# Seven block products in place of eight in the SwiGLU down-projections of a two-layer hybrid trunk

## The chip, the cores and the metric

The kernel runs on one core of one Trainium2 chip. The metric is the device time of one execution in microseconds (us), as a median of several runs. TensorE (PE) multiplies, VectorE (DVE) and ScalarE (ACT) work on rows of 128 partitions, GpSimd (POOL) does elementwise work and issues accumulating DMAs, SyncE (SP) issues plain loads.

## The reference

Two layers over x of 512 positions by 1024 features, in float32. Each layer is a SwiGLU stage, a token-mixing stage (recurrent branch, short convolution, sparse attention) and a second SwiGLU stage:

```
def swiglu(x, w_gate_up, w_down):
    g, u = jnp.split(x @ w_gate_up, 2, axis=-1)
    return (jax.nn.silu(g) * u) @ w_down

for l in range(DEPTH):                                   # DEPTH = 2
    x = x + 0.5 * swiglu(rms_norm(x, ffn1_norm[l]), ffn1_w_gate_up[l], ffn1_w_down[l])
    x = x + token_mixing(rms_norm(x, mix_norm[l]), ...)
    x = x + 0.5 * swiglu(rms_norm(x, ffn2_norm[l]), ffn2_w_gate_up[l], ffn2_w_down[l])
return rms_norm(x, final_norm)
```

D_MODEL is 1024 and D_FF is 2816, so a down-projection maps 22 chunks of 128 hidden rows to 8 chunks of 128 features, and there are four of them.

## The kernel before

Features lie on the partitions, the 512 positions are the columns. x is held as 8 tiles of 128x512. Float32 accuracy is had with three matmuls for each product of two 128-wide operands (`mm3`, L390 to L392): every operand is cut into a rounded part `hi` and a remainder `lo`, and hi by hi, hi by lo and lo by hi are added up in PSUM.

**The stream of weights.** `Stream` (from L210) brings all weights as 496 units of 128x1024 (eight 128x128 tiles) in the order in which TensorE will use them. A unit is loaded into a raw buffer by SP (L231; five buffers, RAWB), and cut: ScalarE writes minus the raw weight into `wlo` (L251) and the rounded weight into `whi` (L252), and an accumulating DMA issued by POOL (L253) moves `wraw` onto `wlo`. There are three pairs of cut buffers (CUTB): a unit's cut begins when the unit three places ahead of it has been used up.

**A SwiGLU stage** (`ffn`, L517) takes 22 hidden chunks in two halves of 11. Each hidden chunk has a gate and an up projection, each a `chunk` of 8 k-steps (24 matmuls of 512 columns, one weight unit). VectorE evacuates them (L530, L539), ScalarE applies silu (L532), POOL multiplies gate and up (L542), and `cut` (L412 to L418) makes hi and lo of the hidden chunk. After each half come 8 down chunks, one for each x tile, of 11 k-steps (33 matmuls); VectorE adds half of each result to x (L555). After the second half each finished x tile goes to the next norm at once (`Norm.add`): hi and lo of the scaled x (L443 on ScalarE, L444 on VectorE), its square (L451) and the sum of squares on POOL (L460). The next stage's matmuls need seven of its eight x tiles before the first may start (`chunk`, `v_task`).

**The order.** `Sched` runs a list schedule at build time: every task is a generator that yields operations with a cost, a priority and waits; the operation with the lowest priority number that is ready goes next on its engine, and the instructions are issued in this order. The cuts of weights have priority -1e6 and so go ahead of all else on their engines; evacuations of PSUM get a bump of -100; all else has the order number of its task. On the chip each engine then works through its own list in order.

**PSUM** has eight banks: three of kind a (chunks), two s, two t, one o (attention, norms and the value projection). SBUF holds 66 slots of 128x512 (`G`, NSLOT), eight of them x.

Of the kernel before, what the change touches and what calls it, by code (L numbers as in the profile page):

```python
# [20 lines left out]
P = 128  # L21
# [18 lines left out]
NHU = 496  # L40
RAWB, CUTB = 5, 3
NSLOT = 66
# [5 lines left out]
TOPK_AT = 40  # L48

# [159 lines left out]

class Stream:  # L210


    def __init__(self, nc, sch, pool, wall):
        self.nc, self.s, self.pool, self.wall = nc, sch, pool, wall
        self.n = wall.shape[0]
        self.parts, self.order, self.avail = {}, [], 0
        self.raw, self.cut = Res(RAWB), Res(CUTB)

    def task(self, gate):
        for j in range(self.n):  # L220
            if j == 1:
                yield gate
            yield self.raw
            box = {}
            pieces = 4 if j == 0 else 1
            w = 1024 // pieces

            def dma():
                if "raw" not in box:
                    box["raw"] = self.pool.tile([P, 1024], F32, name="wraw", tag="wraw", bufs=RAWB)  # L230
                self.nc.sync.dma_start(box["raw"][:, i * w:(i + 1) * w], self.wall[j][:, i * w:(i + 1) * w])  # L231

            for i in range(pieces):
                yield "sp", 1.46 if j else 0.6, dma, {}
                self.s.spawn(self._cut(j, box["raw"], i * w, w), -1e6 + j)
                if pieces > 1:
                    yield 0.7

    def _cut(self, j, raw, off, w):
        yield 2.0  # L240
        if off == 0:
            yield self.cut
            self.parts[j] = (self.pool.tile([P, 1024], F32R, name="whi", tag="whi", bufs=CUTB),
                             self.pool.tile([P, 1024], F32R, name="wlo", tag="wlo", bufs=CUTB))
        hi, lo = (t[:, off:off + w] for t in self.parts[j])
        src = raw[:, off:off + w]
        if j == 0:
            yield ACT(w, lambda: self.nc.scalar.copy(hi, src))
            yield DVE(w, lambda: self.nc.vector.tensor_sub(lo, src, hi.bitcast(F32)))
        else:  # L250
            yield ACT(w, lambda: self.nc.scalar.mul(lo, src, -1.0))  # L251
            yield ACT(w, lambda: self.nc.scalar.copy(hi, src))  # L252
            yield "pool", 1.0, lambda: self.nc.gpsimd.dma_start(lo, src, accum_op=ALU.add), {}  # L253
            yield 4.0
        if off + w == 1024:
            self.s.release(self.raw)
        self.avail += w // P
# [7 lines left out]
    def half(self, key):  # L265
        j = len(self.order) // 8
        self.order += [key + (r,) for r in range(8)]
        return self.parts.pop(j)

    def tile(self, key):  # L270
        j, r = divmod(len(self.order), 8)
        self.order.append(key)
        hi, lo = self.parts[j]
        if r == 7:
            del self.parts[j]
            self.s._at(self.s.t + 0.7, lambda: self.s.release(self.cut))
        return hi[:, r * P:(r + 1) * P], lo[:, r * P:(r + 1) * P]
# [3 lines left out]
def trunk_kernel(ctx: ExitStack, tc: tile.TileContext, wall, x_in, pos_in, cols_in, out):  # L281
# [10 lines left out]
    W = Stream(nc, sch, wp, wall)  # L292
# [223 lines left out]

    def ffn(name, l, u, xs, nxt):  # L517

        hid = [Part() for _ in range(2 * HF)]
        mid = [Event() for _ in range(KT)]  # L520
        new = [[x, Event()] for x, _ in xs]

        def pair(c, prio):
# [11 lines left out]
            def u_task():  # L535
                ps = yield from chunk((name + "u", l, c), u.u)
                yield u.rev
                t2 = G()
# [3 lines left out]
                yield POOL(S, lambda: O.tensor_mul(t2, box["t"], t2))  # L542
# [607 lines left out]
```

## Time and profile before

| what | us |
|---|---|
| median of three runs | 2962.79 (2962.65 to 2963.1) |
| the profiled execution, its own time | 2961.89 |
| span of the profiled execution, first to last instruction | 2960.0 |
| TensorE busy | 2897.5 (98%), 12720 matmuls |
| VectorE, ScalarE, POOL busy | 955.2 (32%), 1499.6 (51%), 927.6 (31%) |
| mean granted clock of TensorE | 0.987 |

The profile is of one execution, 1.9 us of which lie outside the span. A matmul row gives a start and a modelled duration; matmuls overlap, so the pace is read from the distance of the starts and not from the durations. Times in rows are us from the span's start, means are in ns.

### The profile page before, as it was taken

Reading aid. Unit: us, or ns where it says so; the run is one execution under the profiler, and the core shown is the slowest. Engines: PE = TensorE matmul, PEld = TensorE weight load, DVE = VectorE, ACT = ScalarE, POOL = GpSimd, SP = SyncE. Lnnn points to the kernel's source line nnn. Section 1 sums busy time; section 2 is a strip of 40 time slices with the busy share of each in tenths; the row PEclk is TensorE's granted clock in tenths of the full one; section 3 lists DMA queues with packets and bytes.
Section 4 is the critical chain, followed back from the end, with each engine's and each line's share of the span. In section 5 each row is a group of like instructions: output and inputs, shape, how many; then the busy total and the mean of one; then the engine's idle time right before and its main releaser. Section 6 shows DMA issues by size and latency. Waiting matters only on the chain.

```text
span 2960.0 us, 32761 instructions
## 1 busy us (share of the span) xinstructions
PE 2897.5 (98%) x12720; PEld 2358.5 (80%) x12720; DVE 955.2 (32%) x1699; ACT 1499.6 (51%) x1930; POOL 927.6 (31%) x923
## 2 busy tenths in 40 slices
PE   8999999799999999999999999988999999999998
PEld 6888887678888888888888888877788888888886
DVE  5311148944312222111111111599361231211111
ACT  5534457666533455434544345567664334544443
POOL 2212254543222232212322123646332222322222
PEclk9999999899999999999999999999999999999999
DMA  7888886566688888888888888856657888888885
GB/s 213 188 194 185 188 196 159 132 162 145 138 191 192 190 185 185 187 189 185 193 185 192 184 193 185 199 135 157 159 130 165 186 187 190 186 186 190 191 185 128
DMA packets 145818, 526.29 MB, mean 178 GB/s; under 512 B 16192, under 2 KB 16832, under 8 KB 145664
## 3 DMA queue, kind: packets, MB, share of 16 engines
q0 software_dynamic: 71360, 259.82, 49.0%
q1 hardware_dynamic: 73584, 263.23, 27.7%
q8 instruction: 100, 1.64, 0.2%
q10 hardware_dynamic: 720, 1.17, 0.1%
q14 instruction: 54, 0.44, 0.1%
HBM read 262.53 MB, written 2.10 MB: 89 GB/s over the span
## 4 chain that ended last, share of the span: by engine, by line
PE 90%; DVE 7%; ACT 1%; issue 1%; POOL 1%; DMA 1%; SPq 0%; DVEq 0%; ACTq 0%; POOLq 0%
PE psa L390 29%; PE psa L392 29%; PE psa L391 29%; DVE g L706 1%; DVE m L705 1%; DVE g L731 1%; DVE g L771 1%; PE pst L915 1%; DVE g L770 0%; DVE g L699 0%; DVE g L791 0%; DVE g L728 0%; PE pso L930 0%; DVE g L793 0%; PE pso L931 0%
## 5 line engine op out<-in xcount | busy, mean ns | idle before, releaser
L390 PE MATMUL psa<-g,whi 128*128 128x512 f32 x3920 | 1560.5, 398 | 43.3 <-DVE xr L726 27.9
L391 PE MATMUL psa<-g,whi 128*128 128x512 f32 x3920 | 1556.6, 397 | 6.1 <-POOL g L418 5.8
L392 PE MATMUL psa<-g,wlo 128*128 128x512 f32 x3920 | 1556.0, 397 | 0.8 <-DMA wlo<-wraw 0.8
L251 ACT ACTIVATE wlo<-wraw 128x1024 fp32r<-128x1024 f32 x495 | 524.6, 1060 | 1235.1 <-PE psa L392 1226.3
L390 PEld LDWEIGHTS psa<-g,whi 128*128 128x128 f32 x3920 | 744.6, 190 | 218.6 <-DVE xr L726 23.9
L391 PEld LDWEIGHTS psa<-g,whi 128*128 128x128 f32 x3920 | 744.6, 190 | 177.4 <-POOL g L418 6.7
L392 PEld LDWEIGHTS psa<-g,wlo 128*128 128x128 f32 x3920 | 744.3, 190 | 175.6 <-DMA wlo<-wraw 1.6
L253 POOL DMA_DIRECT2D wlo<-wraw x495 | 429.3, 867 | 1231.7 <-ACT wlo L251 1148.2
L252 ACT CAST whi<-wraw 128x1024 fp32r<-128x1024 f32 x495 | 511.3, 1033 | 0.0
L542 POOL TENSOR_TENSOR g<-g 128x512 f32<-128x512 f32 x88 | 114.2, 1297 | 358.4 <-DVE g L539 347.0
L416 DVE TENSOR_TENSOR g<-g 128x512 fp32r<-128x512 f32 x142 | 102.7, 723 | 267.3 <-ACT g L414 267.0
L539 DVE TENSOR_TENSOR g<-psa,g 128x512 f32<-128x512 f32 x88 | 60.8, 691 | 379.4 <-PE psa L392 379.4
L555 DVE SCALAR_TENSOR_TENSOR x<-psa,x 128x512 f32<-128x512 f32 x64 | 44.3, 692 | 384.3 <-PE psa L392 384.3
L414 ACT CAST g<-g 128x512 fp32r<-128x512 f32 x174 | 107.8, 619 | 77.3 <-DVE g L731 32.4
L530 DVE TENSOR_TENSOR g<-psa,g 128x512 f32<-128x512 f32 x88 | 60.9, 692 | 180.4 <-PE psa L392 180.3
L841 POOL TENSOR_TENSOR g<-g 128x512 f32<-128x512 f32 x32 | 41.3, 1290 | 127.9 <-DVE g L838 127.9
L460 POOL TENSOR_TENSOR g<-g 128x512 f32<-128x512 f32 x44 | 57.4, 1304 | 63.1 <-ACT g L451 63.0
L823 DVE TENSOR_TENSOR g<-psa,g 128x512 f32<-128x512 f32 x48 | 33.1, 690 | 127.2 <-PE psa L392 126.6
L838 DVE TENSOR_TENSOR g<-psa,g 128x512 f32<-128x512 f32 x32 | 22.1, 692 | 148.9 <-PE psa L392 148.9
L418 POOL TENSOR_TENSOR g<-g 128x512 fp32r<-128x512 f32 x32 | 47.8, 1492 | 65.6 <-ACT g L414 65.6
L444 DVE SCALAR_TENSOR_TENSOR g<-x,cols,g 128x512 fp32r<-128x512 f32 x48 | 35.8, 751 | 70.0 <-ACT g L443 70.0
L532 ACT ACTIVATE g<-g 128x512 f32<-128x512 f32 x88 | 55.0, 626 | 0.6 <-DVE g L530 0.6
(185 smaller groups left out, 1714.4 us busy)
## 6 DMA issues: line engine op xcount, KB each, us to landing
wraw<-in_w_dram SPq DMA_DIRECT2D x495, 512.0 KB, 4.2
wlo<-wraw POOLq DMA_DIRECT2D x495, 512.0 KB, 5.7
x<-in_x_dram SPq DMA_DIRECT2D x8, 256.0 KB, 4.6
out_dram<-g ACTq DMA_DIRECT2D x4, 256.0 KB, 2.9
out_dram<-g SPq DMA_DIRECT2D x4, 256.0 KB, 3.1
wraw<-in_w_dram SPq DMA_DIRECT2D x4, 128.0 KB, 4.5
posi<-in_pos_dram POOLq DMA_DIRECT2D x1, 256.0 KB, 5.1
cols<-in_cols_dram ACTq DMA_DIRECT2D x1, 118.0 KB, 3.3
```

The lines of the kernel that those rows point to most:

```text
L251: yield ACT(w, lambda: self.nc.scalar.mul(lo, src, -1.0))
L252: yield ACT(w, lambda: self.nc.scalar.copy(hi, src))
L253: yield "pool", 1.0, lambda: self.nc.gpsimd.dma_start(lo, src, accum_op=ALU.add), {}
L390: T.matmul(ps, wh, xh, start=first, stop=False)
L391: T.matmul(ps, wh, xl, start=False, stop=False)
L392: T.matmul(ps, wl, xh, start=False, stop=last)
L414: yield ACT(S, lambda: A.copy(part.h, src))
L416: yield DVE(S, lambda: V.tensor_sub(part.lo, src, part.h.bitcast(F32)))
L460: yield POOL(S, lambda: O.tensor_add(self.acc, self.acc, s))
L530: yield DVE(S, lambda: V.tensor_mul(t, ps, u.R), bump=EVAC)
L539: yield DVE(S, lambda: V.tensor_mul(t2, ps, u.R), bump=EVAC)
L542: yield POOL(S, lambda: O.tensor_mul(t2, box["t"], t2))
```

## The change

The down-projection is regrouped. The 22 hidden chunks are taken in blocks of 8, 8 and 6, and after the gate and up chunks of a block comes its part of the down-projection, as two *quads* (four x tiles each). In a quad weights and hidden activations are seen as 2x2 blocks: rows are pairs of x tiles, the inner dimension goes by even and odd hidden chunks, the columns by halves of 256 positions. The seven products of Winograd's form of Strassen's scheme take the place of eight. Each product is a row of matmuls of 256 columns, 24 in an 8-chunk block and 18 in the 6-chunk block, on a sum of weight blocks and a sum of activation blocks:

- Weights: `_quad` loads W11, W22, W12 and W22 again into four raw buffers (RAWB is six now); two DMAs on POOL add W21 from memory onto a raw buffer, two VectorE additions make the other sums, and each of the seven is cut into `whi` (ScalarE copy) and `wlo` (VectorE subtraction). One `_cutter` hands out the three pairs of cut buffers in the order of PLAN, which fixes where quads stand among the 408 plain units that are left.
- Activations: `Pair.make` makes seven forms (hi and lo) for each pair of hidden chunks.
- Outputs: three accumulators in PSUM, x in bank s, y in o and z in t. z goes on adding over the products 0, 2, 4 and 6 and is copied out (ScalarE) after 0 and 2; y is copied after product 1. VectorE adds the pieces to x. Two x tiles of a quad are final after product 5, two after product 6.
- x tiles lie in four persistent tiles of 128x1024 instead of eight slots; NSLOT is 58. The product of gate and up moves from POOL to VectorE.

```
-RAWB, CUTB = 5, 3
-NSLOT = 66
+RAWB, CUTB = 6, 3
+NSLOT = 58
+BLOCKS = ((0, 8), (8, 16), (16, 22))
...
+            for _b, (_c0, _c1) in enumerate(BLOCKS):
+                PLAN += ["s"] * (2 * (_c1 - _c0)) + [(_part, _l, _b, _q) for _q in range(2)]
...
+        def sums(t11, t22, t12):                    # in _quad
+            yield 1.0
+            yield "pool", 0.9, lambda: O.dma_start(t22, w21, accum_op=ALU.add), {}
+            yield 5.0
+            s.set(us1.src)
+            yield us1.ev
+            yield DVE(w, lambda: V.tensor_add(t22, t22, t11), ap=1)
+            s.set(us2.src)
+            s.spawn(third(t11), prio + 1)
+            yield us2.ev
+            yield u12.ev
+            yield DVE(w, lambda: V.tensor_add(t22, t22, t12), ap=1)
+            s.release(self.raw)
+            s.set(us4.src)
...
+        def third(t11):
+            yield u11.ev
+            yield "pool", 0.9, lambda: O.dma_start(t11, w21, accum_op=ALU.add), {}
+            yield 5.0
+            s.set(us3.src)
...
+    def _cutter(self):
+        for k, u in enumerate(self.units):
+            yield u.src
             yield self.cut
...
+        elif u.plain is not None:
+            yield ACT(u.w, lambda: A.mul(u.lo, u.raw, -1.0))
+            yield ACT(u.w, lambda: A.copy(u.hi, u.raw))
+            yield "pool", 0.9, lambda: O.dma_start(u.lo, u.raw, accum_op=ALU.add), {}
...
         else:
+            yield ACT(u.w, lambda: A.copy(u.hi, u.raw))
+            yield DVE(u.w, lambda: V.tensor_sub(u.lo, u.raw, u.hi.bitcast(F32)), ap=1)
...
+        def make(self, a, b):                       # in Pair
+            yield ACT(H, lambda: A.copy(ab[:, :H], a1))
+            yield DVE(H, lambda: V.tensor_sub(ab[:, H:], a1, ab[:, :H].bitcast(F32)))
...
+            yield DVE(H, lambda: V.tensor_sub(t1, a1, a2), ap=1)
+            yield DVE(H, lambda: V.tensor_sub(t3, b2, a2), ap=1)
+            yield DVE(H, lambda: V.scalar_tensor_tensor(t2, t1, -1.0, b2, op0=ALU.mult, op1=ALU.subtract), ap=1)
+            yield DVE(H, lambda: V.scalar_tensor_tensor(t4, t2, -1.0, b1, op0=ALU.mult, op1=ALU.subtract), ap=1)
+            for src, i, j in ((t, 3, 4), (u, 5, 6), (b, 2, 1)):
+                h, lo = G(F32R), G(F32R)
+                yield ACT(S, lambda: A.copy(h, src))
+                yield DVE(S, lambda: V.tensor_sub(lo, src, h.bitcast(F32)))
...
+    STEPS = ((0, 0, "z", True), (1, 3, "y", True), (2, 5, "z", False), (3, 1, "x", True), (4, 4, "z", False),
+             (5, 2, "y", False), (6, 6, "z", False))
...
+            yield u.ev                              # in product(i)
+            yield pairs[0].ev[form]
+            if before:
+                yield seen[before[-1]]
...
+                    for m in range(2):
+                        o = acc[z][:, m * H:(m + 1) * H]
...
+                        T.matmul(o, u.hi[:, c], xh, start=begin and k == 0 and m == 0, stop=False,
...
+                yield PE(6 * 262, go)
+            W.used()
...
-                yield POOL(S, lambda: O.tensor_mul(t2, box["t"], t2))
-                yield from cut(hid[c], t2)
+                yield DVE(S, lambda: V.tensor_mul(t2, box["t"], t2))
+                sch.set(hev[c])
...
+                yield done[5]                       # in evac
+                yield add(x12, acc["y"], 0.5, bump=EVAC)
+                sch.release(banks[QBANK["y"]])
+                last = b == len(BLOCKS) - 1
+                for r in range(2):
+                    m = 4 * q + r
+                    if last:
+                        sch.set(new[m][1])
+                        nxt.add(m, new[m][0], prio + r)
+                yield done[6]
+                yield add(x21, acc["z"], -0.5, bump=EVAC)
...
+            for q in range(2):
+                p = tick() + 8 * q
+                was[q] = [spawn(down(b, q, was[q], p), p)]
+                seq[0] += 4
```

## Rows read from the trace of the kernel before

**Rows 1.** The page: busy time by engine, the granted clock, the chain by engine.
```profile
PE 2897.5 (98%) x12720; PEld 2358.5 (80%) x12720; DVE 955.2 (32%) x1699; ACT 1499.6 (51%) x1930; POOL 927.6 (31%) x923
...
PEclk9999999899999999999999999999999999999999
...
PE 90%; DVE 7%; ACT 1%; issue 1%; POOL 1%; DMA 1%; SPq 0%; DVEq 0%; ACTq 0%; POOLq 0%
```

**Rows 2.** Timeline, VectorE, a down-projection: start, duration, instruction, idle before, its releaser.
```profile
150.78 0.69 DVE L555 SCALAR_TENSOR_TENSOR x<-psa,x 128x512 f32<-128x512 f32 x1 [4.12 <-PE psa L392]
158.46 0.69 DVE L555 SCALAR_TENSOR_TENSOR x<-psa,x 128x512 f32<-128x512 f32 x1 [6.98 <-PE psa L392]
```

**Rows 3.** Stretch of seven down chunks: length, busy by engine, PEclk, DMA share, GB/s.
```profile
150.60:204.40 53.80, 53.80 (x233) 43.65 (x232) 4.84 (x7) 18.07 (x19) 8.03 (x10) 1.00 0.81 193
```

**Rows 4.** Timeline, TensorE and its weight loads, in the value projection (264 columns).
```profile
388.42 0.28 PE L636 MATMUL psa<-whi,g 128*128 128x264 f32 x1
...
392.55 0.28 PE L637 MATMUL pso<-wlo,g 128*128 128x264 f32 x1
...
388.43 0.19 PEld L637 LDWEIGHTS psa<-wlo,g 128*128 128x128 f32 x1
388.55 0.19 PEld L635 LDWEIGHTS psa<-whi,g 128*128 128x128 f32 x1
```

**Rows 5.** One weight cut on ScalarE and POOL (timeline), and L253's DMAs (its line).
```profile
148.69 1.06 ACT L251 ACTIVATE wlo<-wraw 128x1024 fp32r<-128x1024 f32 x1 [2.76 <-PE psa L392]
149.66 1.03 ACT L252 CAST whi<-wraw 128x1024 fp32r<-128x1024 f32 x1
...
150.05 0.86 POOL L253 DMA_DIRECT2D wlo<-wraw  x1 [3.97 <-ACT wlo L251]
...
DMA to landing us min/median/max: 4.5/5.7/8.7
```

**Rows 6.** VectorE by line and form: count, busy us, mean ns, idle before.
```profile
L416 DVE TENSOR_TENSOR g<-g 128x512 fp32r<-128x512 f32 x142 | 102.7, 723 | 267.3 <-ACT g L414 267.0
L444 DVE SCALAR_TENSOR_TENSOR g<-x,cols,g 128x512 fp32r<-128x512 f32 x48 | 35.8, 751 | 70.0 <-ACT g L443 70.0
L920 DVE TENSOR_TENSOR g<-pst,g 128x512 fp32r<-128x512 f32 x16 | 11.0, 686 | 9.7 <-ACT g L919 9.7
L920 DVE TENSOR_TENSOR g<-pst,g 128x256 fp32r<-128x256 f32 x16 | 6.8, 423 | 11.3 <-ACT g L919 11.3
```

**Rows 7.** ScalarE by line and form, with the same columns.
```profile
L414 ACT CAST g<-g 128x512 fp32r<-128x512 f32 x174 | 107.8, 619 | 77.3 <-DVE g L731 32.4 <-DVE g L793 24.9 <-POOL g L542 16.3
L443 ACT ACTIVATE g<-x,cols 128x512 fp32r<-128x512 f32 x48 | 34.3, 719 | 24.1 <-DVE x L555 22.4 <-DMA cols<-in_cols_dram 1.3
L451 ACT ACTIVATE g<-x 128x512 f32<-128x512 f32 x56 | 34.0, 618 | 16.7 <-DVE x L555 16.6
L919 ACT CAST g<-pst 128x256 fp32r<-128x256 f32 x16 | 5.8, 364 | 5.6 <-PE pst L915 5.5
```

**Rows 8.** Timeline, ScalarE and VectorE, where the first stage ends.
```profile
388.50 1.06 ACT L251 ACTIVATE wlo<-wraw 128x1024 fp32r<-128x1024 f32 x1 [3.57 <-PE psa L392]
...
390.40 0.72 ACT L443 ACTIVATE g<-x,cols 128x512 fp32r<-128x512 f32 x1
...
388.50 0.69 DVE L555 SCALAR_TENSOR_TENSOR x<-psa,x 128x512 f32<-128x512 f32 x1 [5.42 <-PE psa L392]
391.16 0.75 DVE L444 SCALAR_TENSOR_TENSOR g<-x,cols,g 128x512 fp32r<-128x512 f32 x1 [1.96 <-ACT g L443]
```

**Rows 9.** Stretches around pauses of TensorE, with the columns of rows 3.
```profile
566.00:569.00 3.00, 0.28 (x2) 0.14 (x1) 2.93 (x8) 2.97 (x5) 1.91 (x3) 0.85 0.69 131
569.00:575.00 6.00, 6.00 (x15) 4.68 (x16) 5.83 (x11) 3.95 (x6) 4.32 (x4) 0.50 0.74 181
...
30.00:40.00 10.00, 9.10 (x53) 7.59 (x52) 3.41 (x9) 4.17 (x6) 0.85 (x1) 1.00 0.57 131
```

**Rows 10.** Timeline, the end of the kernel.
```profile
2944.93 0.69 DVE L555 SCALAR_TENSOR_TENSOR x<-psa,x 128x512 f32<-128x512 f32 x1 [6.97 <-PE psa L392]
...
2946.33 1.09 PE L480 MATMUL pss<-ones,g 128*128 128x1 f32 x8 [0.66 <-ACT g L451]
```

More of the change, by code (lines that the diff above doesn't have):

```diff
@@ L217, in __init__ @@
         self.raw, self.cut = Res(RAWB), Res(CUTB)
-    def task(self, gate):
[L220 to L237, printed above, removed]
@@ L239, in _cut @@
-    def _cut(self, j, raw, off, w):
-        yield 2.0
-        if off == 0:
-            yield self.cut
[L243 to L249, printed above, removed]
-        else:
[L251 to L255, printed above, removed]
+        self.units, self.plain, self.quads = [], [], {}
@@ new lines, in __init__ @@
+        for e in PLAN:
+            if e == "s":
+                u = Unit(plain=len(self.plain))
+                self.plain.append(u)
+                self.units.append(u)
+            else:
+                self.quads[e] = [Unit(quad_width(e)) for _ in range(7)]
+                self.units += self.quads[e]
+    def task(self, gate):
+        self.s.spawn(self._cutter(), -1e6)
+        n = 0
+        for e in PLAN:
+            if e == "s":
+                if n == 1:
+                    yield gate
+                yield from self._plain(self.plain[n])
+                n += 1
+            else:
+                yield from self._quad(e)
@@ new lines, in _later, with _load, _plain @@
+    def _later(self, ev, t):
+        self.s._at(self.s.t + t, lambda: self.s.set(ev))
+    def _load(self, src):
+        yield self.raw
+        t = self.pool.tile([P, 1024], F32, name="wraw", tag="wraw", bufs=RAWB)[:, :src.shape[1]]
+        yield "sp", 1.46, lambda: self.nc.sync.dma_start(t, src), {}
+        return t
+    def _plain(self, u):
+        src = self.wall[u.plain]
+        if u.plain:
+            u.raw = yield from self._load(src)
+            self._later(u.src, 2.0)
+            return
+        yield self.raw
+        u.raw = self.pool.tile([P, 1024], F32, name="wraw", tag="wraw", bufs=RAWB)
+        for i in range(4):
+            p = slice(i * 256, (i + 1) * 256)
+            yield "sp", 0.6, lambda: self.nc.sync.dma_start(u.raw[:, p], src[:, p]), {}
+            if i == 0:
+                self._later(u.src, 2.0)
+            yield 0.7
@@ L517, in ffn, with chunk_pair @@
+    QBANK = {"x": "s", "y": "o", "z": "t"}
     def ffn(name, l, u, xs, nxt):
-        hid = [Part() for _ in range(2 * HF)]
-        mid = [Event() for _ in range(KT)]
+        NC = FF // P
+        hid = [None] * NC
+        hev = [Event() for _ in range(NC)]
+        pairs = [Pair() for _ in range(NC // 2)]
         new = [[x, Event()] for x, _ in xs]
-        def pair(c, prio):
+        def chunk_pair(c, prio):
             gate, box = Event(), {}
```

207 lines of the change are left out of this document (167 added, 40 removed).

## Prediction, made before the changed kernel ran

> **What bounds the kernel now.** I read the page first: TensorE is busy for 98% of the span, its clock is granted in full in nearly every slice, and 90% of the chain that ended last is TensorE [rows 1]. So fewer matmul-us are worth their length, as long as TensorE goes on being fed. Then the timeline of a down-projection: VectorE adds one finished chunk to x every 7.67 us [rows 2] (16 such rows a stage, 64 in all, at the same distance), with 33 matmuls between two of them, 0.2324 us for 512 columns. In seven such chunks TensorE is busy for every one of 53.8 us while VectorE has 4.84 and ScalarE 18.07 us of work [rows 3]: no wait to win there, but much room on the other engines. One weight unit lasts 24 x 0.2324 = 5.58 us. The rest of this text is on what happens when a unit lasts only half as long and needs other engines more.
>
> **The work on TensorE.** Removed: 64 x 7.67 = 490.9 us (2112 matmuls). Added: 24 quads (three blocks, two quads, four stages), 16 of 7 x 24 matmuls and 8 of 7 x 18, together 3696 of 256 columns. The nearest row is the value projection with 264 columns: 34 steps in 392.55 - 388.42 = 4.13 us, 0.1215 each [rows 4]; scaled to 256 columns 0.1178. Ends: 0.1162 (half of 0.2324) and 0.1215 (no gain from fewer columns). I take 0.1178, as each of these matmuls brings its own weight load just like the quads': 435.4 us (429.5 to 449.1). TensorE wins 55.5 us (41.8 to 61.4). A product lasts 24 x 0.1178 = 2.83 us, in the last block 18 x 0.1178 = 2.12 us.
>
> **Weight loads.** A load row shows 0.19 us, yet two loads start 0.12 us apart [rows 4]: they overlap, so they set no floor of 0.19. [...]
>
> **The way out of a quad.** Three pairs of cut buffers mean that a unit's cut starts when the unit three ahead is used up, two products before its turn: 2 x 5.58 = 11.2 us now, 5.66 behind a quad. For a plain unit that is short: ScalarE 1.06 us, POOL issues 1.36 us after ScalarE began, and the data land 5.7 us later (4.5 to 8.7) [rows 5]; with about 0.3 us for the last matmul to end and for the last wait, 7.4 us. The third matmul is the first to need wlo, 0.46 us in. So TensorE waits 7.4 - 5.66 - 0.46 = 1.3 us on leaving the blocks of 8, eight times: +10.6 us (4 to 20). Behind the last block it is 2.7 us, under the wait for the norm below.
>
> **The way in.** The last pair's forms begin when the block's last chunk ends: about 0.2 us of latency, two VectorE operations of 0.69 (the evacuation; the gate product, now on VectorE), then 0.42 for the first form's remainder, four sums of 0.42, three remainders of 0.69 [rows 6], with ScalarE copies of 0.36 and 0.62 between them [rows 7]. Between these the list puts the cut of the third unit (1.2 us, the 512-column row with 0.53 more for 512 columns), since cuts go first. Form 0 comes at 3.4 us, form 3 at 7. The other pairs' steps of products 0 and 1 fill 6 x 0.71 = 4.2 us, so form 0 costs nothing; then z must be copied out on ScalarE before product 2 may add to it, about 0.9 us with nothing else ready. In the last block only four steps fill (2.8 us): 2 us. Sum: 8 x 1.0 + 4 x 2.0 = +16 us (6 to 34).
>
> **Inside.** Each product asks 1.2 us of VectorE for wlo, 0.69 for an addition to x, and two sums of weights in seven products, 1.2 each: 15.7 us against 19.8 us of a quad on TensorE. The 6-chunk block has 0.95 us for 768 columns: 13.4 against 14.8. With 5.6 us of the last pair's forms and 3 us for the first quad's norm (4 x 0.75, [rows 6]) both its quads ask 35.4, less 2.9 done ahead, against 29.7 and 2.0 of waiting: 0.8 over, and I take 1.5 for queueing, four times: +6 us (0 to 16). Waits that are new: product 2 for the copy of z, 4 for the next copy, 6 for a VectorE addition; behind each stands all of TensorE, but one product (2.1 or 2.8 us) lies between and they need about 1. S3 needs a DMA from memory that waits for VectorE's sum; behind it in POOL's list stand the next cuts' DMAs. In the second quad it is ready at about 9.6 us of the 11.3 at which product 4 starts (last block 8.7 of 8.5), with 5.7 us for the DMA, nothing in the sum. The first quad starts its DMA long before. SP's list holds 504 loads instead of 496 and waits for raw buffers only; TensorE waits for no load of it.
>
> **The ends of stages.** Now the last x tile's norm is hidden: its evacuation at 388.50 stands beside a weight cut on ScalarE, the tile follows at 390.40 and VectorE ends at 391.91 [rows 8], while the next stage multiplies the seven tiles that it has. After the change two tiles finish with product 5 and two with product 6, and seven of eight are needed. ScalarE has, from 2.1 us before the end, a plain cut to finish (to about -0.1), tile 4 (0.72), another plain cut (2.0), the square of 4 (0.62), tile 5 and its square (1.34), tile 6 (0.72) [rows 5, 7], and VectorE 0.75 [rows 6]: the next stage starts 6.4 us after product 6, where the bare chain (0.2 + 0.69 + 0.72 + 0.75 and latencies) would take 2.7. [...] Three ends of 8.9: +26.7 us (9 to 36). The fourth is the kernel's: today only one tile's square is open between the last addition (2944.93) and the last sums (2946.33) [rows 10]; with four tiles open the POOL sums of squares come behind them: +4 us (2 to 6).
>
> **Costed at nothing.** ScalarE loses 88 double cuts and gains 168 single ones and 72 copies of z and y, all below 60% in a quad. POOL loses 88 products to VectorE, hidden by the next chunk (11 us a pair). The slots lose eight that x no longer needs. The mixing stages keep their work; another order in their lists can move their waits by some 5 us either way.
>
> **Sum.** -55.5 + 10.6 + 16 + 6 + 26.7 + 4 = +7.8. On the profiled execution's 2961.9 that is 2969.7, and the median of the runs lies 0.9 above that execution: **2970 us**. With its own terms at moderate size this case runs from 2957 to 2985.
>
> **Rivals.**
> Cheap seams, faster. The seams are worked out from lists that I traced by priority alone. If ScalarE takes the tiles ahead of the cuts (4 us an end with a little clock, 12), the DMAs land near 4.5 us (exits 3), forms are mostly covered (entries 7, inside 0) and the tail costs 3, then -55.5 + 25 = -30: 2932. For it: VectorE and ScalarE are nearly empty before a quad [rows 3], so work can run ahead. Against it: row 390.40 shows a tile standing behind a weight cut already [rows 8].
> The DMA that makes S3, slower. It decides from a landing of 7.4 us on (5.5 in the last block). At the 8.7 us that L253's longest took [rows 5], the second quads wait 1.3 us eight times and 3.2 four times, +23: 2993. Against it: that is the longest of 495, and DMA gets less to do in quads. For it: the source is memory and not SBUF, which no row shows.
> [...]
> Weight loads as a floor. If 0.19 us [rows 4] did not overlap, 3696 x 0.19 = 702 in place of 435: 3237. The distance of the loads speaks against it.
>
> **Chances.** Forecast 0.40; cheap seams 0.33; S3 0.18; half clock 0.07; loads 0.02. About 0.2% (5.9 us) is what a measurement of this kernel can tell from no change. The forecast's case lies half within it and half above: faster 0.33, same 0.20, slower 0.47. For 8 in 10 the range takes in cheap seams and the DMA with the bounds of TensorE's pace: 2928 to 3005; the forecast's own is 2957 to 2985.
>
> **What would show it.** In the profile after: starts of 256-column matmuls 0.118 us apart; about 1 us of TensorE idle at the start of each first quad, released by ScalarE or VectorE; 1.3 us before the first chunk behind each second quad, released by the DMA of wlo; 6 us after each stage, released by VectorE (L444's successor), then a stretch at 0.5; VectorE near 1450 us busy (168 remainders 188, 48 sums 54, 168 additions 116, 44 pairs' forms 184, 88 gate products 61, less 88 x 0.72 and 64 x 0.69, on the 955 of [rows 1]). I am wrong in the pace if the starts lie 0.16 or more apart, wrong in the seams if TensorE idles under 30 us more in the SwiGLU stages than now, and wrong about VectorE if product after product waits for wlo inside quads.

## The result and the profile after

The changed kernel takes 2984.07 us (median of 4 runs, 2982.64 to 2984.55) beside 2962.94 of the kernel before (2962.65 to 2963.74): ratio 1.0070, 95% interval 1.0053 to 1.0088. It is slower by 21 us, where the prediction had 2970 in a range of 2928 to 3005 and gave "slower" the largest chance. The profiled execution took 2984.55 us with a span of 2982.8, 22.8 more than the span before.

The page of the kernel after: busy time by engine, the chain by engine, and three groups of DMA issues (KB each, median us from issue to landing).

```profile
PE 2874.0 (96%) x14304; PEld 2407.7 (81%) x14304; DVE 1430.8 (48%) x2371; ACT 1541.4 (52%) x2076; POOL 791.6 (27%) x795
...
PE 78%; DVE 11%; issue 6%; DMA 3%; POOL 1%; ACT 1%; SPq 0%; DVEq 0%; POOLq 0%; ACTq 0%
...
wlo<-wraw POOLq DMA_DIRECT2D x407, 512.0 KB, 5.9
...
wraw<-in_wq_dram POOLq DMA_DIRECT2D x32, 512.0 KB, 7.0
...
wraw<-in_wq_dram POOLq DMA_DIRECT2D x16, 384.0 KB, 5.7
```

Set beside [rows 1]: TensorE is busy for 23.5 us less, and yet the span is longer. Its share of the chain fell from 90% to 78%, and VectorE, the DMA and plain issue took what it lost. The other engines became links where they had been company.

TensorE's own waits in the kernel after (us in total, times, longest):

```profile
PE psa L504 <- DMA wlo<-wraw: 20.2, 13, 4.8
PE pst L693 <- ACT g L761: 17.1, 8, 4.2
...
PE psa L880 <- DMA wlo<-wraw: 6.0, 2, 3.1
PE pso L696 <- DVE wlo L364: 5.9, 8, 0.7
PE pst L696 <- DVE wlo L364: 5.7, 4, 1.4
```

L693 and L696 are matmuls of the quads, L504 those of plain chunks, L880 the value projection. All five groups are new with the change, but for one wait of 0.8 us in the first.

**The account.** The pace is as foreseen. Two TensorE rows inside a quad of the kernel after:

```profile
389.28 0.28 PE L693 MATMUL pst<-g,whi 128*128 128x256 f32 x1
...
390.94 0.29 PE L696 MATMUL pst<-g,wlo 128*128 128x256 f32 x1
```

These are 14 steps in 1.66 us, 0.1186 each (0.1178 was taken), so the 3696 matmuls need 438.3 us in place of 490.9. Measured from its first matmul to the first of the next chunk, an 8-chunk block's part (336 matmuls) takes 41.43 to 41.55 us where the pace asks 39.85, and the last block's (252 matmuls) 36.84, 39.15, 39.28 and 39.37 where it asks 29.9. All twelve together take 486.4 us. So the quads gain 4.5 us on the old down chunks, and 48.1 us of waits, and of slow clock behind them, stand inside.

| term | predicted, us | measured, us |
|---|---|---|
| matmuls of the quads at their pace | -55.5 | -52.6 |
| waits inside quads, 8 blocks of 8 | +8 (way in) | +13.1 |
| waits inside quads, 4 last blocks | +14 (way in 8, inside 6) | +35.1 |
| ways out of the blocks of 8 | +10.6 | +6.1 |
| three stage ends (with shifts in the mixing stages) | +26.7 | +16.1 |
| end of the kernel | +4 | +3.9 |
| start | 0 | +1.3 |
| sum | +7.8 | +23.0 (span +22.8) |

The stage ends here are what the mixing stages and the start of the second layer are longer by; part of it are mixing waits that changed places when the list was made anew, which I did not take apart.

**The stall in the last block.** TensorE's timeline in the second quad of the first stage (start, duration, in brackets idle time before and its releaser), then ScalarE, VectorE and POOL around it:

```profile
372.62 0.28 PE L696 MATMUL pso<-g,wlo 128*128 128x256 f32 x1
377.05 0.54 PE L693 MATMUL pst<-g,whi 128*128 128x256 f32 x1 [4.14 <-ACT g L761]
...
374.43 1.56 ACT L363 CAST whi<-wraw 128x768 fp32r<-128x768 f32 x2 [2.52 <-DVE wraw L306]
375.90 0.62 ACT L563 ACTIVATE g<-x 128x512 f32<-128x512 f32 x1
376.43 0.56 ACT L761 COPY g<-pst 128x512 f32<-128x512 f32 x1
...
369.06 0.74 DVE L556 SCALAR_TENSOR_TENSOR g<-x,cols,g 128x512 fp32r<-128x512 f32 x1
369.72 0.95 DVE L364 TENSOR_TENSOR wlo<-wraw,whi 128x768 fp32r<-128x768 f32 x1
370.59 1.78 DVE L556 SCALAR_TENSOR_TENSOR g<-x,cols,g 128x512 fp32r<-128x512 f32 x1
372.30 2.02 DVE L306 TENSOR_TENSOR wraw<-wraw 128x768 f32<-128x768 f32 x1
...
370.25 3.25 POOL L572 TENSOR_TENSOR g<-g 128x512 f32<-128x512 f32 x2 [18.99 <-ACT g L563]
```

Read it backwards. Product 2 adds onto z and waits for the copy of z (L761). ScalarE makes that copy late: it stands in its list behind the rounding of a sum of weights (L363), and ScalarE idles 2.52 us there for the sum itself (L306 on VectorE). L306 took 2.02 us, and the L556 ahead of it 1.78, while the same L556 had taken 0.74 just before. What began in between is POOL's sums of squares for the next norm (L572, from 370.25 on). Over all calls L556 has a mean of 0.976 us in the kernel after, where the same operation had 0.751 [rows 6].

The rows speak for turns and not for half speed: L556 and L306 are longer by 1.04 and 1.07 us, and one sum of POOL takes 1.27 us where no operation of VectorE stands beside it (18.81 us). In the second SwiGLU stage the same meeting goes the other way, and it is POOL's sum that is stretched (first row, 3.91 us), while VectorE keeps its lengths:

```profile
1476.09 3.91 POOL L572 TENSOR_TENSOR g<-g 128x512 f32<-128x512 f32 x1 [1.18 <-ACT g L563]
...
1476.72 0.68 DVE L756 SCALAR_TENSOR_TENSOR x<-g,x 128x512 f32<-128x512 f32 x1
1477.32 0.94 DVE L311 TENSOR_TENSOR wraw<-wraw 128x768 f32<-128x768 f32 x1
```

Spans on POOL are rough, so this is an inference. Operations of VectorE that read PSUM kept their length beside POOL (L756 at 2943.52 us, 0.69; L832 has a mean of 0.684 in the 12 calls beside POOL and of 0.691 in the 18 others). The trace of the kernel before holds the same meeting, in the mixing stage: L416 takes 0.69 us in the 134 calls without an operation of POOL beside them, and here

```profile
1880.31 2.22 DVE L416 TENSOR_TENSOR g<-g 128x512 fp32r<-128x512 f32 x1 [1.07 <-ACT g L414]
...
1880.38 1.59 POOL L594 TENSOR_TENSOR g<-g,si 128x512 f32<-128x512 f32 x1
```

So the longer lengths could have been read before the change.

What the pause does to the clock, as windows of the kernel after (stretch, length, busy by engine PE, PEld, DVE, ACT, POOL, PEclk, DMA share, GB/s):

```profile
372.00:377.00 5.00, 0.90 (x8) 0.69 (x6) 5.00 (x6) 2.57 (x5) 2.70 (x3) 1.00 0.18 14
377.00:383.00 6.00, 5.95 (x37) 5.95 (x38) 4.22 (x5) 2.47 (x4) 1.51 (x1) 0.72 0.58 140
391.00:394.00 3.00, 0.47 (x4) 0.26 (x3) 1.35 (x2) 3.00 (x5) 1.20 (x2) 1.00 1.05 198
394.00:397.00 3.00, 2.59 (x12) 2.59 (x12) 2.21 (x2) 3.00 (x7) 2.63 (x2) 0.53 1.06 183
```

The mean of 0.72 holds two levels: the clock is 0.50 from 378 to 380 us, where matmuls of 256 columns start 0.213 us apart (12 steps in 2.56 us from 377.60 on), and 1.00 from 381 to 383, where they start 0.120 apart (10 steps in 1.20 us from 380.69 on). The first pair is the stall above: six us at 0.72, about 1.7 lost (6 x 0.28, an estimate), follow. With the first quad's entry (0.84 and 0.46), this stall, 1.57 for a remainder (L364) and the clock, that block's 9.4 us are accounted for. The second pair is the end of the stage: 3 us of hardly any TensorE work, then a clock of 0.53.

### The profile page after: what moved, and what is told of

Its sections match the earlier page's. It is cut to its first block, busy times and chain, and to the rows that moved or that the text cites. A ratio compares the mean times of both kernels' runs of the same rounds, so it can differ in the third digit from the quotient of the medians.

```text
span 2982.8 us, 36980 instructions
## 1 busy us (share of the span) xinstructions
PE 2874.0 (96%) x14304; PEld 2407.7 (81%) x14304; DVE 1430.8 (48%) x2371; ACT 1541.4 (52%) x2076; POOL 791.6 (27%) x795
## 4 chain that ended last, share of the span: by engine, by line
PE 78%; DVE 11%; issue 6%; DMA 3%; POOL 1%; ACT 1%; SPq 0%; DVEq 0%; POOLq 0%; ACTq 0%
PE psa L504 23%; PE psa L502 22%; PE psa L503 22%; DMA wlo<-wraw 3%; DVE g L949 2%; DVE m L948 2%; PE pst L693 1%; PE pst L696 1%; PE pst L695 1%; DVE g L1034 1%; DVE g L974 1%; DVE wlo L364 1%; DVE g L1014 1%; PE pso L696 1%; DVE wraw L306 1%
## 5 line engine op out<-in xcount | busy, mean ns | idle before, releaser
L502 PE MATMUL psa<-g,whi 128*128 128x512 f32 x3216 | 1283.4, 399 | 37.9 <-DVE xr L969 15.5
L504 PE MATMUL psa<-g,wlo 128*128 128x512 f32 x3216 | 1280.6, 398 | 20.2 <-DMA wlo<-wraw 20.2
L503 PE MATMUL psa<-g,whi 128*128 128x512 f32 x3216 | 1278.7, 398 | 0.3 <-DVE g L556 0.3
L502 PEld LDWEIGHTS psa<-g,whi 128*128 128x128 f32 x3216 | 611.0, 190 | 185.7 <-DVE xr L969 9.2
L504 PEld LDWEIGHTS psa<-g,wlo 128*128 128x128 f32 x3216 | 610.6, 190 | 171.3 <-DMA wlo<-wraw 26.4
L503 PEld LDWEIGHTS psa<-g,whi 128*128 128x128 f32 x3216 | 610.7, 190 | 140.9 <-DVE g L556 1.3
L363 ACT CAST whi<-wraw 128x1024 fp32r<-128x1024 f32 (+1 forms) x168 | 159.8, 977 | 228.4 <-PE psa L503 97.1
L693 PE MATMUL pst<-g,whi 128*128 128x256 f32 x704 | 203.7, 289 | 18.9 <-ACT g L761 17.1
L696 PE MATMUL pst<-g,wlo 128*128 128x256 f32 x704 | 200.7, 285 | 5.7 <-DVE wlo L364 5.7
L695 PE MATMUL pst<-g,whi 128*128 128x256 f32 x704 | 200.9, 285 | 0.0
L364 DVE TENSOR_TENSOR wlo<-wraw,whi 128x1024 fp32r<-128x1024 f32 (+1 forms) x168 | 186.1, 1133 | 29.0 <-ACT whi L363 28.9
L693 PEld LDWEIGHTS pst<-g,whi 128*128 128x128 f32 x704 | 134.9, 192 | 25.0 <-ACT g L761 20.2
L696 PEld LDWEIGHTS pst<-g,wlo 128*128 128x128 f32 x704 | 135.0, 192 | 6.5 <-DVE wlo L364 6.5
L695 PEld LDWEIGHTS pst<-g,whi 128*128 128x128 f32 x704 | 135.2, 192 | 0.6
L319 POOL DMA_DIRECT2D wraw<-in_wq_dram x24 | 20.8, 867 | 345.0 <-DVE wraw L306 192.2
L696 PE MATMUL pso<-g,wlo 128*128 128x256 f32 x352 | 100.1, 284 | 5.9 <-DVE wlo L364 5.9
```

The source lines that it names most:

```text
L363: yield ACT(u.w, lambda: A.copy(u.hi, u.raw))
L364: yield DVE(u.w, lambda: V.tensor_sub(u.lo, u.raw, u.hi.bitcast(F32)), ap=1)
L502: T.matmul(ps, wh, xh, start=first, stop=False)
L503: T.matmul(ps, wh, xl, start=False, stop=False)
L504: T.matmul(ps, wl, xh, start=False, stop=last)
L693: T.matmul(o, u.hi[:, c], xh, start=begin and k == 0 and m == 0, stop=False, skip_group_check=True)
```

## The experiments

Ratios are to the kernel before on the same chip, with 95% intervals; each edit is on the changed kernel unless said otherwise. Two theories stand at first. A: POOL's sums of squares make VectorE's operations about twice as long, and ScalarE's order passes the delay on to TensorE. B: VectorE simply has too much to do, or data come too late for the short products, wherever POOL is.

**e1_hold_sums.** The sums of squares on POOL wait for the last product of the stage.

```diff
             elif late or self.cutting or self.count < KT:
+                if self.go:
+                    yield self.go
                 yield POOL(S, lambda: O.tensor_add(self.acc, self.acc, s))
...
+                if last and q and nxt.go:
+                    sch.set(nxt.go)
```

> Edit: the sums of squares on POOL for the next norm (L572) wait until the stage's last product is done; nothing is left out. Theory A (collision): in the second quad of a stage's last block VectorE's two-input operations run beside POOL's sums at about twice their length (L306 2.02 us for 0.95, L556 1.78 for 0.75), which delays the weight sum, on which ScalarE stands while the copy of z is queued behind it. Then L306 and L556 return to 0.95 and 0.75 there, the wait of TensorE for L761 falls from 4.2 to about 1.2 us, the last blocks from 39.3 to about 35 us, and the kernel gains 4 x 4 = 16 us on 2984: 2966 to 2972. Theory B (lookahead): the cuts come late because three pairs of cut buffers are too few, whatever POOL does: 2982 to 2986.

Measured: 2972.62 us, ratio 1.0036 (1.0024 to 1.0048), just above what theory A had. The gain is 10 us by the ratios, 12.0 by the spans (2970.8). The last blocks take 34.3 to 35.6 us. VectorE's timeline at the same place, the window that answers to the stall, and TensorE's wait for the copy of z:

```profile
371.75 0.75 DVE L557 SCALAR_TENSOR_TENSOR g<-x,cols,g 128x512 fp32r<-128x512 f32 x1
372.42 0.95 DVE L306 TENSOR_TENSOR wraw<-wraw 128x768 f32<-128x768 f32 x1
```

```profile
372.00:377.00 5.00, 2.96 (x23) 2.76 (x24) 5.00 (x8) 4.14 (x7) 0.87 (x1) 1.00 0.32 37
```

```profile
PE pst L696 <- ACT g L764: 10.7, 8, 2.0
```

The same operations on the same data are at 0.75 and 0.95 again; TensorE has 2.96 us of work in the five where it had 0.90. That is theory A. The meeting itself is not gone: POOL's sums now meet the next norm's tiles behind the stage, and the mean of L557 (L556 without the edit) is 1.005 us beside 0.976. What the edit takes away is its place inside the quads. And 5 us a block and a 2.0 us wait for z remain, so B has a share: with a full list, VectorE and ScalarE still deliver late.

**e2_six_first.** The short block goes first: the collision should then meet a block whose products last longer.

```diff
-BLOCKS = ((0, 8), (8, 16), (16, 22))
+BLOCKS = ((0, 6), (6, 14), (14, 22))
```

> Edit: the blocks are (0,6), (6,14), (14,22) instead of (0,8), (8,16), (16,22), so that the 18-matmul quads stand first in a stage, without a norm beside them, and 24-matmul quads last. Theory A (VectorE is over-full in the short quads only together with the norm): the 6-chunk blocks fall from 39.3 us to 32 to 33, the last blocks of 8 rise from 41.5 to at most 43; 2984 - 4 x (6.5 - 1.5) = 2964, range 2958 to 2972. Theory B (lookahead, a property of short products): the 6-chunk blocks keep most of their 9.6 us over the pace: 2976 to 2984.

Measured: 2989.18 us (2982.24 to 2991.76, the profiled execution 2982.24), ratio 1.0085 (1.0056 to 1.0113): no gain, and above both expectations. VectorE in the last block of the first stage:

```profile
370.12 2.12 DVE L306 TENSOR_TENSOR wraw<-wraw 128x1024 f32<-128x1024 f32 x1
372.15 3.13 DVE L556 SCALAR_TENSOR_TENSOR g<-x,cols,g 128x512 fp32r<-128x512 f32 x2
```

The short blocks become cheap (33.5 to 33.9 us, but for the very first with 37.8), and the collision goes with the end of the stage: there a block of 8 now takes 44.47 us. The exits from short blocks cost more as well (TensorE's waits of plain chunks for wlo: 23.1 us against 20.2). So the stall comes with what else runs at the end of a stage; the width of the block sets how much of it TensorE feels (4.6 us over the pace here, 9.4 in the short block).

**e3_exit_cut.** The first plain unit behind each pair of quads is cut like a quad's, without a DMA.

```diff
+        elif u.plain is not None and u.quick:
+            yield ACT(u.w, lambda: A.copy(u.hi, u.raw))
+            yield DVE(u.w, lambda: V.tensor_sub(u.lo, u.raw, u.hi.bitcast(F32)), ap=1)
```

> Edit: the first plain weight unit behind each pair of quads is cut by a ScalarE copy and a VectorE subtraction (about 2.7 us) instead of two ScalarE operations and a DMA (7.4 us). If the waits for the DMA of wlo behind the quads (0.4 to 1.0 us eight times, 2.6 to 3.2 us three times, and the slow clock after the long ones) are a matter of that latency alone, they vanish: 6 + 9 + about 4 = 19 us, 2963 to 2970. Rival: at the stage ends the norm of the last x tiles is as late as the DMA, as the prediction had it (6.4 us after product 6): then only the eight short waits go, 2976 to 2980.

Measured: 2984.93 us, ratio 1.0072 (1.0049 to 1.0095), no change, where both expectations had a gain. The waits of plain chunks for wlo fall from 13 to 4 (12.2 us, mostly in the mixing stages), so their cause at the exits is the DMA's landing. But one group of TensorE's waits grew:

```profile
PE pss L599 <- POOL g L579: 8.6, 3, 3.4
```

At the end of a stage TensorE reaches the sums of the norm sooner and waits for POOL there. The next wait takes the place of the one removed.

**e4_four_pairs.** A fourth pair of cut buffers (paid with four slots), so that a cut may begin one unit earlier.

```diff
-RAWB, CUTB = 6, 3
-NSLOT = 58
+RAWB, CUTB = 6, 4
+NSLOT = 54
```

> Edit: four pairs of cut buffers instead of three (CUTB 4), paid with four slots (NSLOT 54). Theory B (lookahead): each cut starts one product earlier, all waits of TensorE for wlo (DMA and VectorE) go, and the stall for the copy of z with them, as the weight sums on which ScalarE stood are made earlier: 51 + 6 + 13 us of losses shrink to under 20, 2984 - 45 = 2939, range 2930 to 2950. Theory A (collision and VectorE's load): waits for the DMA go (19 us), the stall for z in the last blocks stays: 2960 to 2968.

Measured: 2973.7 us, ratio 1.0040 (1.0024 to 1.0056), above both expectations. TensorE's waits for the DMA of wlo shrink to one of 4.9 us at the kernel's start, the last blocks to 38.0 (the kernel's last to 34.1), the blocks of 8 stay at 41.3 to 41.7. Again POOL's sums come next (TensorE's timeline, second layer):

```profile
1494.53 1.30 PE L592 MATMUL pss<-ones,g 128*128 128x1 f32 x8 [2.06 <-POOL g L572]
```

The run shows one thing more. With the cut earlier, ScalarE copies z at 372.11 us, ahead of the weight sum that it had stood behind, while VectorE's operations are as long as in the kernel after (L556 1.79 us, L311 2.04). No wait of TensorE for that copy is left, but one for a remainder of VectorE comes in its place:

```profile
372.11 0.56 ACT L761 COPY g<-pst 128x512 f32<-128x512 f32 x1
374.24 0.83 ACT L363 CAST whi<-wraw 128x768 fp32r<-128x768 f32 x1 [0.84 <-DVE wraw L311]
...
378.89 0.48 PE L696 MATMUL pso<-g,wlo 128*128 128x256 f32 x1 [2.04 <-DVE wlo L364]
```

**e5_sums_split.** The squares of the four tiles that finish last are summed on VectorE instead of POOL.

```diff
+            if fast and self.last is None:
+                self.last = s
+            elif fast:
+                yield DVE(S, lambda: V.tensor_add(self.last, self.last, s))
```

> Edit: at a stage's end the squares of x tiles 4 to 7 are summed on VectorE instead of POOL (tiles 0 to 3 stay on POOL), and the matmuls with ones take two sums. Theory: the last tiles' sums on POOL (1.3 to 1.8 us each, in a row) stand in the kernel's tail and, once the wait for wlo is gone, at the stage ends. In this kernel the wait for wlo is still there, so only the tail shrinks, 19.2 to about 16.5 us, and the stage ends stay: 2979 to 2983. Rival (what POOL does in the second quad is the whole of the collision, and half of its sums still stand there): the last blocks keep 39 us. If the last blocks fall to 36, half of the sums already make the collision harmless: 2968.

Measured: 2990.22 us, ratio 1.0099 (1.0078 to 1.0119), above the expectation. The kernel's end gains 1.1 us, but the sums' matmuls now stand inside the quads and wait for VectorE (5.2 us in three waits); the last blocks take 40.7 to 41.5, the kernel's last 37.8. Taken alone the edit costs.

**e6_product_on_pool.** One part of the change undone: the product of gate and up is on POOL again.

```diff
-                yield DVE(S, lambda: V.tensor_mul(t2, box["t"], t2))
+                yield POOL(S, lambda: O.tensor_mul(t2, box["t"], t2))
```

> Edit: the product of silu(gate) and up goes back to POOL (1.3 us each, 88 of them), the rest of the change stays. Theory A (VectorE's work when a quad starts sets the entry, 2 us on each 8-chunk block): VectorE has two operations less before the forms but POOL's takes 0.6 us longer, so the entry is 0.5 us later at most; 2984 to 2992. Rival (VectorE's total load, 1431 us, is the bound): 61 us less of it give 10 us or more: under 2976.

Measured: 2993.85 us, ratio 1.0111 (1.0091 to 1.0131). VectorE has 88 operations fewer, and TensorE's wait for the copy of z grows to 22.4 us in 16 places. So VectorE's total is not the bound. This part of the change is right as it stands.

**e7_four_pairs_hold_split.** e4 and e5 together, with POOL's sums held until product 3 of the stage's last quad.

> Edits: four pairs of cut buffers (NSLOT 54), sums of squares of tiles 0 to 3 on POOL held until product 3 of the stage's last quad is done, of tiles 4 to 7 on VectorE. If the three causes are separate (lookahead, collision, POOL's sums at the ends), their gains add: from 2974 with four pairs alone the last blocks fall from 37.9 to 35 (-12), the waits for POOL's sums at the ends go (-6), the tail loses 2: 2950 to 2958, below the kernel before. If each wait only makes room for the next one: 2962 to 2970.

Measured: 2958.65 us, ratio 0.9993 (0.9984 to 1.0003). Alone the fourth pair had given -0.3% (e4), holding the sums -0.3% (e1, held a little longer) and the split +0.3% (e5); together they give -0.8%; last blocks 33.7 us. That is just above the sum of the gains that was expected. The mean of L556's successor is 0.749 us: no VectorE operation of that line meets POOL's sums any more. Three additions to x do (2.56 us each for 0.69), but TensorE waits at most 1.0 us for an addition to x. What is left at the ends of stages, as a timeline row and the window behind it:

```profile
1482.62 1.86 PE L601 MATMUL pss<-ones,g 128*128 128x1 f32 x8 [1.77 <-DVE g L570]
```

```profile
1484.00:1488.00 4.00, 4.00 (x12) 3.23 (x12) 0.83 (x5) 0.20 (x1) 0.00 (x0) 0.50 0.98 304
```

TensorE has matmuls of the next stage that need none of this sum, but they stand behind it in its list, and then four us pass at half clock.

**e8_six_first_four_pairs.** e2 on top of e7.

> Edits: as in the run with four pairs, held and split sums, and the blocks (0,6), (6,14), (14,22). With the collision out of the way the last block has VectorE work of about 40 us against 39.6 of TensorE instead of 35 against 29.7, so it should come to 41.5 to 42.5, the 6-chunk block to 32 to 33.5 (both its quads without a norm): 116 us a stage instead of 118, four times 2: 2 to 10 us below the run with the same edits and the short block last. If the norm's place is not what makes the short block dear, no difference within 2 us.

Measured: 2979.99 us, ratio 1.0065 (1.0048 to 1.0081), worse than e7 by 21 us, where 2 to 10 less or no difference were expected. TensorE behind a short pair of quads, as a timeline row and the window behind it:

```profile
1223.41 0.50 PE L504 MATMUL psa<-g,wlo 128*128 128x512 f32 x1 [3.96 <-DMA wlo<-wraw]
```

```profile
1224.00:1228.00 4.00, 4.00 (x12) 3.13 (x11) 0.00 (x0) 0.00 (x0) 0.00 (x0) 0.57 1.06 228
```

A product of 18 matmuls (2.1 us) leaves the first plain cut too little time, and behind the pause the clock is at 0.57. The step on the way out had 2.7 us for the exit from a short block and let the wait for the norm cover it; inside a stage there is no such cover, and the wait is 4 us here (11.4 us in four such waits; e7 has 0.5 behind its quads, not counting the value projection). The waits for the last sum have grown as well, from 6.9 us to 13.9.

**e9_late_sums.** e7, with the stage's last sum 5 us later in TensorE's list.

```diff
             yield self.sev
+            if self.split and self.cutting:
+                yield 5.0
             if self.two:
```

> Edit on top of the run with four pairs, held and split sums: the last matmuls with ones of a stage's norm are put about 5 us later into TensorE's list. Theory: at the stage ends TensorE stood 1.4 to 2.3 us at these small matmuls for VectorE's sum of squares, with the next stage's matmuls behind them in its list, and then ran some 4 us at half clock; both go, three times 3 to 4 us: 2946 to 2950 against 2958. If another wait takes the place (wlo of the next unit, or the tiles themselves): 2954 to 2959.

Measured: 2950.44 us, ratio 0.9958 (0.9941 to 0.9975). TensorE's waits for that sum, in e7 and then here, where only the one at the kernel's end is left:

```profile
PE pss L601 <- DVE g L570: 6.9, 4, 2.3
...
PE pss L601 <- DVE g L570: 2.3, 1, 2.3
```

The small matmuls moved out of the way of work that was ready.

**e10_late_sums_exit_cut** (e9 and e3) and **e11_six_first_all** (e10 and e2).

> The last edit and, on top, the exit cut (ScalarE copy and VectorE subtraction for the first plain unit behind each pair of quads). With four pairs the waits for the DMA of wlo behind the quads are short (6.5 us twice over the kernel and 1.5 at the value projection); if they are what is left at the seams, 3 to 8 us less than the run without this edit: 2940 to 2946. If VectorE is full there, none.

> The same edits with the blocks (0,6), (6,14), (14,22). In the run with the short block first, TensorE stood about 4 us for the DMA of wlo behind each short pair of quads (lookahead of three products of 2.1 us against a cut of 7.4 us) and then ran at half clock, though the quads themselves were 1 us a stage shorter. Theory: with the exit cut that wait goes and this order is as good as the other or 4 us better: 2938 to 2946. Rival: what made it slow is something else, and it stays above 2960.

Measured: 2948.48 us, ratio 0.9950 (0.9936 to 0.9965), and 2947.24 us, ratio 0.9946 (0.9931 to 0.9961). e10 falls a little short of what was expected of it, e11 too. Two windows of e10 at the place where e7 had its half clock:

```profile
1474.00:1480.00 6.00, 6.00 (x36) 5.21 (x35) 3.96 (x7) 6.00 (x10) 2.32 (x3) 1.00 1.07 219
1480.00:1486.00 6.00, 6.00 (x32) 4.95 (x31) 1.45 (x4) 3.67 (x5) 0.86 (x1) 1.00 0.95 244
```

No pause, full clock. With the exit mended and the sums later the short block first no longer hurts. e8 had waited longer in both, 11 us more at the exits than e7 and 7 at the sums; no run parts them. e11 beats both kernels, by 0.5% and 1.2%.

**e12_no_last_forms.** The last pair of each block takes the forms of the pair before, so VectorE and ScalarE make none for it.

```diff
+            if any(2 * i + 2 == c1 for _, c1 in BLOCKS):
+                for j in range(7):
+                    yield pairs[i - 1].ev[j]
+                    pairs[i].f[j] = pairs[i - 1].f[j]
+                    sch.set(pairs[i].ev[j])
+            else:
+                yield from pairs[i].make(hid[2 * i], hid[2 * i + 1])
```

> Edit on the changed kernel: the last pair of each block takes the forms of the pair before it; its own sums, copies and remainders (5 ScalarE or VectorE operations of 256 columns and 6 of 512, made when the quad starts) are left out. Theory (the way in is VectorE's work of the last pair): the waits at the start of the quads go (TensorE for wlo 0.74 us in the 8-chunk blocks, for the copies of z 0.68 and 0.30 in the short ones) with what follows them, 8-chunk blocks from 41.45 to 40.0 and the short ones by 1.5 to 2, as VectorE's backlog before the second quad shrinks too: 8 x 1.4 + 4 x 2 = 19 us, 2962 to 2970. Rival (the weight sums and their cuts alone set the way in): the 8-chunk blocks stay above 41 us: 2980 to 2985.

Measured: 2967.73 us, ratio 1.0024 (1.0011 to 1.0038). Six of the eight blocks of 8 take 39.87 us, which is 336 x 0.1187: nothing waits in them any more (the other two take 40.3). The stretch in which a first quad had its wait, in the kernel after and then in this one:

```profile
120.00:125.00 5.00, 4.26 (x36) 4.05 (x35) 4.78 (x6) 3.67 (x5) 0.00 (x0) 1.00 0.56 152
```

```profile
120.00:125.00 5.00, 5.00 (x44) 5.00 (x43) 3.76 (x5) 2.00 (x3) 0.00 (x0) 1.00 0.81 225
```

The wait that is gone stood behind VectorE (kernel after):

```profile
123.64 0.39 PE L696 MATMUL pso<-g,wlo 128*128 128x256 f32 x1 [0.74 <-DVE wlo L364]
```

So the 1.6 us that such a block loses come from the last pair's forms, VectorE's and ScalarE's together, as the edit leaves out both. The last blocks stay at 37.3 to 39.5 (the kernel's last at 34.9 for 36.8): their loss is another one, the collision. L364 takes 2.07 us beside POOL there, and although the copy of z comes early in this run, TensorE stands for that remainder:

```profile
369.84 0.58 PE L696 MATMUL pso<-g,wlo 128*128 128x256 f32 x1 [2.74 <-DVE wlo L364]
```

The lengths of the stages, from landmarks that all traces have (first matmul of the value projections, end of the second SwiGLU stages, last quad):

| kernel | ffn1, layer 1 | mixing | ffn2 | ffn1, layer 2 | mixing | ffn2 | end |
|---|---|---|---|---|---|---|---|
| before | 388.3 | 725.1 | 369.7 | 369.8 | 722.1 | 369.7 | 15.3 |
| after | 391.1 | 728.0 | 371.3 | 375.5 | 729.4 | 368.4 | 19.1 |
| e1 | 387.2 | 728.9 | 365.8 | 372.0 | 731.1 | 366.3 | 19.6 |
| e4 | 387.7 | 730.7 | 368.1 | 372.8 | 730.1 | 364.2 | 19.7 |
| e7 | 383.6 | 729.4 | 363.4 | 370.3 | 729.9 | 363.8 | 18.0 |
| e10 | 384.5 | 725.7 | 364.7 | 365.4 | 725.0 | 364.1 | 17.6 |

In e10 each SwiGLU stage is 4 to 6 us shorter than before and the first mixing stage is level with it; 2.9 us in the second and 2.3 at the kernel's end remain. Of the 55.5 us foreseen from fewer and shorter matmuls, 13 (by the spans) reach the time.

## Why the prediction was right and wrong

- **Bound and pace: right.** TensorE is still the longest engine, its starts in a quad lie 0.1186 us apart (0.1178 forecast), and loads set no floor: rows of 0.19 us each, they start 0.119 us apart there (16 steps in 1.90 us from 388.92 on), and the rival with 3237 is gone. VectorE is busy for 1430.8 us, where 1450 were forecast.
- **Way in: right in mechanism, too small, with another releaser.** 1.6 us for each block of 8 against 1.0; 1.0 of it is lost at the first wait. The waiting matmul stands mostly behind the remainder of a sum of weights on VectorE (L364, up to 0.74 us, eight times), not behind the copy of z. e12 shows that the last pair's forms are what holds it up.
- **Inside: the step that failed.** I costed the last blocks at 14 us, way in and inside together; they lose 35. The step counts VectorE's demand in lengths taken from [rows 6], means of rows with little beside them, and finds it 0.8 us over what a quad offers. It then puts the sums of squares on POOL only at the kernel's end. In fact those sums begin inside the second quad, VectorE's L306 takes 2.02 us instead of 0.95 and L556 1.78 instead of 0.74, and ScalarE, which works in order, holds the copy of z behind the sum that it needs from VectorE. The step says that each product needs about 1 us for such a copy and has a product's time for it; the copy came 4.14 us too late. e1 takes the overlap away, and 10 to 12 us with it. I had looked at each engine's queue by length and not at who waits in whose list.
- **Ways out: right in mechanism, oversized.** Eight waits of 0.23 to 0.86 us for wlo, 6.1 in all with what surrounds them, for 10.6 (the prediction's 1.3 us eight times is 10.4). e3 shows the releaser.
- **Stage ends: right in place, wrong in the wait.** About 3 us of pause each (3.10, 2.60 and 3.22) and then half clock, not 6.4: TensorE's list goes on with the tiles that are ready, and wlo's DMA, not the norm, ends the wait. The 8.9 us that the sum has for an end hold 2.5 for slow clock, an estimate from 15 matmuls in six us at 0.50 [rows 9] (6 - 15 x 0.2324); no run shows that term at an end, and behind the first one 14 steps of the kernel after took 3.23 us (394.41 to 397.64), 1.5 more than 14 x 0.1215. Behind the wait for wlo stood POOL's sums (e3, e4), and behind these VectorE's (e7): three waits (about 3, 2.06 and 1.77 us in the rows shown), one hidden by the other.
- **End of the kernel: right.** 3.9 us for 4.
- **The rival with S3's DMA** did not come about. The page's 7.0 us (5.7 in the last block) mix two lines; S3's is L319, and the other one, L302, starts S1. Landing times of L319, then of L302, over all widths:

```profile
DMA to landing us min/median/max: 4.7/5.4/6.9
...
DMA to landing us min/median/max: 6.3/7.4/9.2
```

S3's stayed under its threshold of 7.4 us, in the last blocks with 4.7 to 5.1 under the 5.5 there, and no wait of TensorE was traced to it.
- **The rival with cheap seams** was wrong for this kernel, but e10 goes some way to it: with order and buffers mended the seams cost 42 us (55.5 less the 13.1 by which its span is shorter) rather than 78. That rival had 25.
- **Half clock, a chance of 0.07,** was wrong as a loss at every seam: 0.74 us of waiting left the clock at 1.00 (120 to 125 us). Longer pauses cost it in most places, but not by their length alone, as the last section shows.

The direction came out right with a sum that was 15 us short, and that it is not further off is luck: the last blocks alone lost 21 us more than forecast, the blocks of 8, the pace and the start another 9, and the ends of stages and the ways out, priced 15 too high, made up for half of it. (The sum's last line, 2969.7 + 0.9, is 2970.6 and not 2970.)

How the 4 us of the stall divide between the long operations and ScalarE's order was not tried by itself, but three runs bear on it. With POOL held back and the order as it was, the wait is 2.0 us (e1); with the copy of z ahead and POOL left alone, TensorE waits 2.04 us (e4) and 2.74 us (e12) for a remainder of VectorE. So each of the two costs 2 us or more by itself, as far as runs can tell that differ in other things too. What makes VectorE and POOL take turns, if they do, was not looked for beyond the overlap itself.

## What to carry to other kernels

A change that makes the bounding engine's steps shorter must be priced in every other engine's time at the new step, with the lengths that operations have *beside each other*: look in the trace for the same operation at two lengths, and see what ran next to it. The trace before had L416 at 0.69 and 2.22 us. Follow an engine's list and not its load: here ScalarE idled 2.52 us for a weight sum with the copy of z behind it in its list, and that copy of 0.56 us cost TensorE 4.14. At a seam several waits of like length hid one another; removing one showed nothing (e3, 2984.93 us), removing all together paid (e9 to e11, 2950.44 to 2947.24).

## What the hardware did that was not expected

- VectorE operations with two inputs in SBUF took 1.04 to 1.53 us longer in the rows above while POOL worked on SBUF tiles: 128x768 at 2.02 us for 0.95, 128x512 at 1.78 for 0.74 and (before) 2.22 for 0.69; with POOL held back they took 0.95 and 0.75 at the same place. Where VectorE kept its lengths beside POOL's addition (0.68 and 0.94 us, from 1476.72 on), the addition took 3.91 us, for a median of 1.28.
- Two accumulating DMAs from memory with the same sizes differed: a median of 5.4 us for one line and 7.4 for the other, against 5.9 for 512 KB from SBUF. Why was not looked for.
- After waits of 0.74 us the granted clock stayed at 1.00; after 1.77 us among one-column matmuls it was 0.50 for 4 us, after 2.94 us 0.53 for 3 us, after 3.96 us 0.57 for 4 us. The length of the wait alone did not decide it: behind two waits of 2.04 us, in e1 and then in e4, the windows are

```profile
377.00:383.00 6.00, 5.97 (x50) 5.76 (x49) 5.31 (x8) 2.89 (x4) 0.00 (x0) 1.00 0.63 165
...
379.00:384.00 5.00, 5.00 (x30) 5.00 (x31) 2.51 (x4) 1.39 (x2) 0.03 (x1) 0.66 0.91 210
```

In the five us that end with the wait TensorE was busy for 2.97 in e1 and for 2.43 in e4.
